# LayerNorm of eight blocks in the convolution's own layout, and raw queries normalised where they are used: a hybrid encoder layer on one core

## The chip, the core and the metric

The kernel runs on one core of a Trainium2 chip. The core's engines run at the same time, each through its own list of instructions in order: PE (TensorE: matrix products and transposes), DVE (VectorE), ACT (ScalarE) and POOL (GpSimd). SP (SyncE) issues all loads and stores of this kernel from one list; 16 DMA engines carry them out. Engines wait for one another by semaphores. SBUF holds tiles of 128 partitions; PE writes its results into PSUM banks of 128 x 512 floats. The metric is the time on the device of one execution, in microseconds (us).

## What is computed

One layer: a first RMSNorm, one projection to seven groups of columns, windowed attention for one half, a convolution with LayerNorm and Silu for the other, gates, and a projection back with a residual. Two sequences of 256 and 2048 rows are 18 blocks of 128 rows.

```python
h = rmsnorm(z, norm_w)
q, k, v, g_att, c_val, c_glu, g_conv = split(h @ w_in)
q = rmsnorm(q by heads, q_norm_w);  k = rmsnorm(k by heads, k_norm_w)
att = windowed_gqa(q, k, v, sink) * silu(g_att)
u = c_val * sigmoid(c_glu)
y = depthwise_conv(u, conv_w, 31 taps) + conv_b
cnv = silu(layernorm(y, ln_w, ln_b)) * silu(g_conv)
out = z + concat(att, cnv) @ w_out
```

## The kernel before

**Stages.** The projection runs over two chunks of the rows, with units of 256 columns that follow one another within a chunk: value and glu of the convolution, the gates, the queries, keys and values. Every product is made in three passes of high and low parts of float32 (`xh`, `xl`), which is why PE is filled. Results that attention needs later go to HBM (`qd` queries, `kd` keys, `vd` values, `gd` gates, `cd` the convolution's output) and are loaded again. In phase 2, which begins within the last queries, the projection's end, the opening of attention and the first products with `w_out` run side by side; after it attention runs alone, in slots: eight slots for each block of 128 rows.

**LayerNorm (`ln_block`).** The convolution leaves `y` with channels on partitions: four tiles of 128 channels. LayerNorm needs sums over channels. So for each block, step `s1` transposes four 128x128 pieces of `y` into a PSUM bank `lnt` (L263), takes mean and variance on DVE (`mv`), and the inverse square root and the shift on POOL (L185, L186, L271). Step `s2` normalises on DVE (`zn`, L281), with rows on partitions. Step `s3` transposes the four pieces of `zn` back (bank `lnu`, L287), and ACT applies weight, bias and Silu (L290); then `zn` is stored to `cd`. `later(n, f)` puts `f` off by n ticks; a tick is a group of matmuls of the main work.

**Queries (`q_group`).** The raw result of a block is copied to a tile `qr` by ACT (L1198), its sum of squares goes to POOL for the inverse root `rqq`, and `fin` multiplies both on DVE (line 490 in the profile, a helper that records the operation) and stores the product to `qd` (L1211). In phase 2 `fin` comes 3 ticks after; for the last four blocks (14 to 17) 10 + 6 x tail ticks more, `put_off`: its products then run at 621 to 676 us, within attention.

**Mixing and output.** Pairs of blocks (p = 0, 1, ...) are taken together, in jobs of sums and differences, each a chain of products into a PSUM bank `yb0` or `yb1` (L755), with tiles `wo0`, `wo1`, ... of the output weights (512 KB a load, L457). A finished bank is added by DVE to the residual in `yo` (`add`, L766) or kept by ACT; the next job that starts the bank waits for it. The tiles `yo0` to `yo3` (256 KB) are loaded by `load_x` (L474) at a slot named in the table `acts`; for the first pair they are at slots 12, 14, 17, 18.

**What sets the order.** Within phase 2 the order on PE and POOL is that of the program. On the other engines, SP's queue among them, a scheduler that simulates the program picks the order, so that a small edit can move a load past others. SP holds its queue while the instruction at the head waits.

## Time and profile before

| | before |
|---|---|
| three runs | 933.9, 935.42, 935.51 us (median 935.42) |
| profiled execution | 935.46 us; span 933.4 |
| bytes moved | 182.79 MB, mean 196 GB/s |
| share of SP's queue in 16 engines' span | 60.0% |

The span is the time from the first to the last recorded instruction; 2.06 us of the execution lie around it. The page cuts the span into 40 slices of 23.3 us; a digit is the busy share in tenths.

```profile
PE   9999999999999999999999999999999999999998
DVE  5799999989988899999996564689788888887884
DMA  8579685488465472223333688998566566576431
GB/s 299 181 226 360 243 287 186 156 272 311 121 211 176 155 290 91 91 99 110 117 116 116 196 268 265 384 361 251 169 171 187 169 200 167 171 187 190 139 96 47
```

Slices 26 and 27 (583 to 630 us) are where DMA moves most: the change of phase. In a row of the timeline stand start, length, engine, line, operation, and in brackets the idle time before it and who ended it.

### The profile page before, as it was taken

The page shows a single profiled execution, that of the slowest core. Times are in us where ns is not written, and L with a number is a line of the kernel's source. Part 1 is how long each engine was busy: PE and PEld are TensorE (multiplying, and loading weights), DVE is VectorE, ACT ScalarE, POOL GpSimd, SP SyncE. Part 2 cuts the span into 40 slices and gives each one's busy share as a digit, 9 for nine tenths or more (in the row PEclk, how much of TensorE's full clock was granted, in tenths as well). Part 3 has the DMA queues.
Part 4 walks back from the last instruction along what each step waited for, and adds up shares of the span by engine and source line. Part 5 has one row for each costly group of instructions (what it writes and reads, how often), then busy time and mean ns, then how long its engine had stood idle before and what let it go on. Part 6 is the DMA issues. An engine that isn't in the chain of part 4 may idle for free.

```text
span 933.4 us, 16976 instructions
## 1 busy us (share of the span) xinstructions
PE 926.0 (99%) x5742; PEld 877.0 (94%) x5742; DVE 786.3 (84%) x1380; ACT 447.6 (48%) x1237; POOL 350.5 (38%) x538
## 2 busy tenths in 40 slices
PE   9999999999999999999999999999999999999998
PEld 8999999999999999999999999988888888888887
DVE  5799999989988899999996564689788888887884
ACT  7441222153447750011111356677667676776772
POOL 3420100075675310000000453676664556455652
PEclk9999999999999999999999999999999999999999
DMA  8579685488465472223333688998566566576431
GB/s 299 181 226 360 243 287 186 156 272 311 121 211 176 155 290 91 91 99 110 117 116 116 196 268 265 384 361 251 169 171 187 169 200 167 171 187 190 139 96 47
DMA packets 154183, 182.79 MB, mean 196 GB/s; under 512 B 48784, under 2 KB 114656, under 8 KB 153968
## 3 DMA queue, kind: packets, MB, share of 16 engines
q1 hardware_dynamic: 154096, 181.71, 60.0%
q8 instruction: 45, 0.74, 0.3%
q14 instruction: 42, 0.34, 0.1%
HBM read 115.81 MB, written 65.85 MB: 195 GB/s over the span
## 4 chain that ended last, share of the span: by engine, by line
PE 97%; DVE 1%; ACT 1%; POOL 1%; issue 0%; DVEq 0%; POOLq 0%
PE pj L1050 43%; PE yb L755 20%; PE pj L1066 16%; PE O L644 5%; PE S L490 4%; PE pT_c L610 2%; PE pT_m L610 2%; PE pT_x L610 1%; PE warmup L1291 1%; PE lnu L287 1%; PE lnt L263 1%; PE qT L490 1%; PE xt L1298 0%; DVE xt L959 0%; DVE y L1131 0%
## 5 line engine op out<-in xcount | busy, mean ns | idle before, releaser
L1050 PE MATMUL pj<-xh,ws 128*128 128x384 f32 (+1 forms) x1536 | 395.4, 338 | 0.1
L1131 DVE SCALAR_TENSOR_TENSOR y<-us,cw,y 128x1167 f32<-128x1167 f32 (+2 forms) x258 | 333.5, 1348 | 0.9
L1050 PEld LDWEIGHTS pj<-xh,ws 128*128 128x128 f32 x1536 | 280.9, 188 | 0.4 <-ACT xh L1306 0.4
L1050 PE MATMUL pj<-xl,ws 128*128 128x384 f32 (+1 forms) x768 | 261.4, 341 | 0.2 <-DVE xl L988 0.2
L1066 PE MATMUL pj<-ws,xh 128*128 128x256 f32 (+1 forms) x880 | 165.4, 284 | 0.7 <-ACT sqq L1179 0.4
L1050 PEld LDWEIGHTS pj<-xl,ws 128*128 128x128 f32 x768 | 144.3, 188 | 0.5 <-DVE xl L988 0.5
L1066 PEld LDWEIGHTS pj<-ws,xh 128*128 128x128 f32 (+1 forms) x880 | 136.5, 187 | 1.4 <-issue 1.0
L755 PE MATMUL yb<-wo,rest 128*128 128x512 f32 (+1 forms) x498 | 132.9, 400 | 0.5 <-DVE rest L490 0.5
L1066 PE MATMUL pj<-ws,xl 128*128 128x256 f32 (+1 forms) x440 | 123.8, 281 | 0.0
L755 PEld LDWEIGHTS yb<-wo,rest 128*128 128x128 f32 x498 | 86.8, 189 | 16.0 <-DVE rest L490 0.9
L580 POOL TENSOR_SCALAR sb<-sb,es 128x304 f32<-128x304 f32 (+4 forms) x144 | 73.0, 525 | 58.4 <-PE pT_x L610 20.6
L1165 ACT ACTIVATE go<-pj 128x384 f32<-128x384 f32 x48 | 23.5, 490 | 147.4 <-PE pj L1050 143.2
L185 POOL TENSOR_SCALAR ssk<-ssk 128x2 f32<-128x2 f32 x18 | 11.8, 657 | 208.2 <-ACT sqk L1179 205.2
L562 ACT ACTIVATE sb<-sb,nm 128x304 f32<-128x304 f32 (+4 forms) x144 | 77.2, 536 | 22.1 <-DVE nm L550 20.2
L550 DVE CUSTOM_DVE_ANT_0 sb<-S,bias,vec 128x304 f32<-128x304 f32 (+4 forms) x144 | 73.3, 510 | 11.4 <-PE S L490 10.4
L1066 PEld LDWEIGHTS pj<-ws,xl 128*128 128x128 f32 (+1 forms) x440 | 82.1, 187 | 0.3
L185 POOL TENSOR_SCALAR ssq<-ssq 128x4 f32<-128x4 f32 (+2 forms) x55 | 27.9, 507 | 99.3 <-ACT xn L913 72.8
L490 PEld LDWEIGHTS S<-kw,q 128*128 128x128 f32 x288 | 52.2, 188 | 11.1 <-ACT rest L490 0.3
L490 PE MATMUL S<-kw,q 128*128 128x304 f32 (+4 forms) x288 | 62.3, 299 | 0.0
L755 PE MATMUL yb<-wo,ptiles 128*128 128x512 f32 x216 | 59.9, 407 | 0.0
L490 POOL TENSOR_TENSOR at<-at,ga 128x256 f32<-128x256 f32 x36 | 27.0, 750 | 79.0 <-DVE at L666 79.0
L766 DVE TENSOR_TENSOR yo<-yb,yo 128x512 f32<-128x512 f32 (+1 forms) x55 | 37.1, 674 | 14.7 <-PE yb L755 14.5
(166 smaller groups left out, 1439.7 us busy)
## 6 DMA issues: line engine op xcount, KB each, us to landing
wd<-ws SPq DMA_DIRECT2D x36, 512.0 KB, 5.8
ws<-wd SPq DMA_DIRECT2D x36, 512.0 KB, 6.1
wraw<-in_w_in SPq DMA_DIRECT2D x52, 256.0 KB, 6.3
xn<-in_z SPq DMA_DIRECT2D x18, 512.0 KB, 5.3
gd<-go SPq DMA_DIRECT2D x48, 192.0 KB, 2.9
yo<-in_z SPq DMA_DIRECT2D x36, 256.0 KB, 3.4
wo<-wod SPq DMA_DIRECT2D x18, 512.0 KB, 7.7
out_y<-yo SPq DMA_DIRECT2D x35, 256.0 KB, 2.3
```

What stands on the lines that cost most here:

```text
L185: nc.gpsimd.tensor_scalar(src, src, scale, eps, op0=ALU.mult, op1=ALU.add)
L490: r = f(*a, **k)
L550: nc.vector.tensor_tensor_reduce(out=sb[:, n, c0:c1], in0=ps[:, 0:w], in1=cst["bias"][:, kv, at + c0 : at + c1], scale=1.0, scalar=nsnk[:, ...
L562: nc.scalar.activation(sb[:, n, c0:c1], sb[:, n, c0:c1], AF.Exp, bias=nm[:, n : n + 1], scale=-1.0, accum_out=rs[:, n : n + 1],)
L580: nc.gpsimd.tensor_scalar(sb[:, k, a0:a1], sb[:, k, a0:a1], es[:, k : k + 1], 1.0, op0=ALU.mult, op1=ALU.mult)
L610: nc.tensor.transpose(pt[: c1 - c0, n, :], sbt[b, kv][:, n, c0:c1], ident)
L644: nc.tensor.matmul(opj[b, kv][:, n0:n1], t, p, start=(k == "c" and i == 0), stop=(k == "x" and i == len(work) - 1),)
L755: nc.tensor.matmul(ps[:, :n], x[mi][:, i, :], w[wi], start=((name, e) in OPENS and k == 0), stop=(done and e == es[-1] and k == 2), skip_g ...
L766: nc.vector.tensor_tensor(y, ps[:, :n], y, op=ALU.add)
L1050: nc.tensor.matmul(ps[:, :n], ws[:, d, wi, P * half_i : P * half_i + P], x[xi][:, d, o : o + n], start=(k == 0), stop=(k == 3 * ND - 1),)
L1066: nc.tensor.matmul(ps[:rows, :UW], x[xi][:, d, o : o + rows], ws[:, d, wi, :], start=(k == 0), stop=(k == 3 * ND - 1),)
L1131: op = nc.vector.scalar_tensor_tensor(y[:, yo + o0 : yo + o1], u[:, o0 + k : o1 + k], cw[:, j, k : k + 1], y[:, yo + o0 : yo + o1], op0=AL ...
```

## The change

For blocks 8 to 15 (`SPREAD`, half-open) LayerNorm is finished in the layout of `y`. `s2` no longer normalises; it transposes two columns of `mv`, each broadcast to 128 columns, so that in a bank every partition holds the 128 rows' factors, and their shifts. `s3` multiplies each of four pieces of `y` by the factors and adds the shifts on DVE; Silu then reads SBUF. For the last four blocks' queries `keep` stores the raw tile one tick after its copy, and `scale_q` multiplies the loaded tile by its `rqq` in slot 3 of the block before.

```diff
+SPREAD = (8, 16)
...
+        spread_b = SPREAD[0] <= b < SPREAD[1]
...
-            later(1, s2)
+            later(2 if spread_b else 1, s2)
 
         def s2():
+            if spread_b:
+                st["rows"] = psum.tile([P, 2, P], F32, tag="d" if phase[0] == 1 else "a", name=f"lnu{b}")
+                for k in range(2):
+                    nc.tensor.transpose(
+                        st["rows"][:, k, :], st["mv"][:, k + 1 : k + 2].to_broadcast([P, P]), ident
+                    )
+                return later(1, s3)
...
         def s3():
-            pt = psum.tile([P, 512], F32, tag="d" if phase[0] == 1 else "a", name=f"lnu{b}")
+            if spread_b:
+                st["zn"] = yp.tile([P, 512], F32, tag="zn", name=f"zn{b}", bufs=4)
+                cn = pt = st["zn"].rearrange("p (j n) -> p j n", n=P)
+                for j in range(NJ):
+                    nc.vector.tensor_tensor(cn[:, j, :], yt[c, j][:, o : o + P], st["rows"][:, 0, :], op=ALU.mult)
+                nc.vector.tensor_tensor(cn, cn, st["rows"][:, 1:2, :].to_broadcast([P, NJ, P]), op=ALU.add)
+            else:
...
+    def scale_q(b):
+        qi, rq = raw_q[b]
+        q = qt[b].rearrange("p a e -> p (a e)")[:, UW * qi : UW * qi + UW].rearrange("p (h e) -> p h e", e=HD)
+        nc.vector.tensor_tensor(q, q, rq.unsqueeze(2).to_broadcast([P, 4, HD]), op=ALU.mult)
...
+        if slot == VSLOT and a + 1 in raw_q:
+            scale_q(a + 1)
...
-                    pin(late and not put_off)(nc.vector.tensor_tensor)(
+                    pin(late)(nc.vector.tensor_tensor)(
...
+                def keep(rq=rq, b=b, raw=raw):
+                    nc.sync.dma_start(qd[b, :, UW * qi : UW * qi + UW], raw.rearrange("p h e -> p (h e)"))
+                    raw_q[b] = (qi, rq)
...
-                later(1 + 2 * late + put_off, fin)
+                if put_off:
+                    later(1, keep)
+                else:
+                    later(1 + 2 * late, fin)
```

The change moves instructions beyond its own lines. A name is a tile with its number, then what is read; lines are those of each kernel's own file (L474 of before is L495 after, L457 is L478, L766 is L787, L755 is L776).

On SP's queue, at the change of phase, before, from the last piece of `wo2` to the load of `yo2`:

```order
L457 DMA wo2_6597<-wod_71 128x1024
L457 DMA wo3_6657<-wod_71 128x1024
L474 DMA yo1_6694<-in_z 128x512
L457 DMA wo3_6657<-wod_71 128x1024 x2
L1211 DMA qd_63<-qr1_13_6456 128x256
L378 DMA q4_7037<-qd_63 128x512
L457 DMA wo5_6881<-wod_71 128x1024
L457 DMA wo4_6780<-wod_71 128x1024
L350 DMA kw1_5913<-kd_65 128x4x32
L457 DMA wo4_6780<-wod_71 128x1024 x2
L474 DMA yo2_6695<-in_z 128x512
```

And after, from the last piece of `wo3` on:

```order
L478 DMA wo3_6676<-wod_71 128x1024
L488 DMA gc3_6963<-gd_64 128x4x128
L488 DMA gc2_7006<-gd_64 128x4x128
L1237 DMA qd_63<-qr1_16_6643 128x256
L392 DMA q4_7055<-qd_63 128x512
L1234 DMA qd_63<-qr1_13_6472 128x256
L478 DMA wo5_6901<-wod_71 128x1024
L478 DMA wo4_6800<-wod_71 128x1024
L364 DMA kw1_5914<-kd_65 128x4x32
L478 DMA wo4_6800<-wod_71 128x1024 x2
L1237 DMA qd_63<-qr1_17_6703 128x256
L495 DMA yo1_6714<-in_z 128x512
```

The load of `yo1` has gone behind everything that stood between it and `yo2`; four raw stores (L1237; those of blocks 14 and 15 stand further up) are newly ahead of it.

On DVE, where the first pair's bank `yb0` is added to `yo1`, before:

```order
L766 TENSOR_TENSOR yo1_6694<-yb0_6725,yo1_6694 128x512 [waits DMAHW3_49,DMAHW1_49,PE_49]
L490 TENSOR_TENSOR rest_6754<-temp1_6768,rest_6754 128x256 [waits Activation_49]
L490 TENSOR_TENSOR rest_6754<-cn0_6262,rest_6754 128x256 [waits DMAHW7_49,Activation_49]
L490 TENSOR_TENSOR ptiles_6207<-cn0_6262,ptiles_6207 128x256 [waits Activation_49]
L666 TENSOR_TENSOR at0_6761<-O0_1_6736,tmp0_1_6858 64x256 [waits Activation_49]
```

and after:

```order
L511 TENSOR_TENSOR rest_6774<-cn1_6274,rest_6774 128x256 [waits Activation_49]
L640 SCALAR_TENSOR_TENSOR ptiles_6223<-pT1_x_0_6890,vec_77,ptiles_6223 128x128 [waits Activation_49]
L640 SCALAR_TENSOR_TENSOR ptiles_6223<-pT1_x_0_6890,vec_77,ptiles_6223 128x128
L511 TENSOR_TENSOR rest_6774<-at0_6781,rest_6774 128x256 [waits Activation_49]
L787 TENSOR_TENSOR yo1_6714<-yb0_6745,yo1_6714 128x512 [waits DMAHW0_49]
L571 ISA sb1_5926,nm2_0_6818<-S2_0_2_6898,bias_5910,vec_77 128x240 [waits PE_49]
```

The addition has moved down past the whole block of `cn0`, `at0` and `cn1`, behind the product with `at0`, and directly waits for a load (DMAHW).

On PE, the job that starts `yb0` anew with `wo1`, before and after:

```order
L606 MATMUL pT1_x_0_6870<-ident_72,pm1_0_6715 128x128 [waits PE_49,Pool_49]
L755 MATMUL yb0_6725<-wo1_6429,ptiles_6207 128x512 [waits Activation_49]
L755 MATMUL yb0_6725<-wo1_6429,ptiles_6207 128x512
L755 MATMUL yb0_6725<-wo1_6429,ptiles_6207 128x512 [waits DVE_49]
L755 MATMUL yb0_6725<-wo2_6597,ptiles_6207 128x512 [waits DMAHW6_49]
```

```order
L627 MATMUL pT1_x_0_6890<-ident_72,pm1_0_6735 128x128 [waits PE_49,Pool_49]
L776 MATMUL yb0_6745<-wo1_6445,ptiles_6223 128x512 [waits DVE_49,Activation_49]
L776 MATMUL yb0_6745<-wo1_6445,ptiles_6223 128x512 x2
L776 MATMUL yb0_6745<-wo2_6615,ptiles_6223 128x512 [waits DMAHW4_49]
L776 MATMUL yb0_6745<-wo2_6615,ptiles_6223 128x512 [waits DMAHW5_49]
```

The job stands at the same place; its first matmul now waits for DVE too, for the count at which the addition above is done.

Also on PE, where block 8's rows are transposed, after:

```order
L265 MATMUL lnt9_5479<-ident_72,y1_3_4745 128x128
L1089 MATMUL pj132_5503<-ws1_8_4971,xh5_3593 128x256 [waits PE_49,Activation_49]
L1089 MATMUL pj132_5503<-ws1_8_4971,xl5_3594 128x256
L1089 MATMUL pj132_5503<-ws1_8_4971,xh5_3593 128x256 x2
L1089 MATMUL pj132_5503<-ws1_8_4971,xl5_3594 128x256
L1089 MATMUL pj132_5503<-ws1_8_4971,xh5_3593 128x256 x2
L1089 MATMUL pj132_5503<-ws1_8_4971,xl5_3594 128x256
L284 MATMUL lnu8_5494<-ident_72,mv8_5428 128x128 [waits DVE_49,Pool_49]
```

Before, `lnu8` waited for DVE (its `zn8`) some eight projection matmuls further down; now it waits for POOL as well.

## The prediction

> **What bounds the kernel now.** First the page: the busy line, then the chain that ended last.

> ```profile
> PE 926.0 (99%) x5742; PEld 877.0 (94%) x5742; DVE 786.3 (84%) x1380; ACT 447.6 (48%) x1237; POOL 350.5 (38%) x538
> PE 97%; DVE 1%; ACT 1%; POOL 1%; issue 0%; DVEq 0%; POOLq 0%
> ```

> TensorE is the bound: 97% of the last chain is PE, and it idles 7 us in the whole span. So anything can only gain by taking PE time away, and anything that makes PE wait costs its full length. Next I cut the span at the stages that the change touches: the rest of the projection with the LayerNorm of chunk 1 (520 to 583 us), the change of phase (581 to 621), and attention up to where the last raw queries will be used. Columns: stretch, length, busy time of PE, PEld, DVE, ACT, POOL, granted clock, DMA share, GB/s.

> ```profile
> 520.00:583.00 63.00, 63.00 (x541) 63.00 (x541) 34.51 (x96) 33.25 (x112) 30.25 (x71) 1.00 0.78 236
> 575.00:578.00 3.00, 3.00 (x28) 3.00 (x27) 1.78 (x5) 0.58 (x3) 1.59 (x5) 1.00 0.41 100
> 581.00:621.00 40.00, 39.38 (x289) 36.46 (x288) 30.32 (x89) 27.61 (x85) 26.90 (x54) 1.00 1.05 386
> 615.30:700.00 84.70, 84.34 (x467) 71.81 (x466) 72.80 (x194) 59.50 (x161) 56.38 (x90) 1.00 0.74 221
> 700.00:840.00 140.00, 140.00 (x792) 120.92 (x791) 118.16 (x308) 100.65 (x263) 75.26 (x107) 1.00 0.64 180
> ```

> PE is full in all of them at a granted clock of 1.00. In the first one DVE and ACT are only a bit over half busy. The third row matters most: for 40 us the DMA engines are full (share 1.05 at 386 GB/s), so there a transfer lands by the bytes ahead of it. Three microseconds before that stretch fills, the share was 0.41.

> **Term 1: PE's transposes.** For blocks 8 to 15 four transposes of zn back become two of the broadcast columns of mv. How much a transpose costs PE is not its duration but the distance to the next start.

> ```profile
> L287 PE MATMUL lnu<-ident,zn x72: 270/272/273, 289.1 to 570.6; 128*128 128x128 f32 x72
> ...
> 540.27 0.28 PE L1066 MATMUL pj<-ws,xl 128*128 128x256 f32 x1
> 540.38 0.60 PE L287 MATMUL lnu<-ident,zn 128*128 128x128 f32 x4
> 540.74 0.36 PE L1066 MATMUL pj<-ws,xh 128*128 128x256 f32 x1
> 540.94 0.60 PE L263 MATMUL lnt<-ident,y 128*128 128x128 f32 x4
> 541.29 0.36 PE L1066 MATMUL pj<-ws,xh 128*128 128x256 f32 x1
> 541.50 0.28 PE L1066 MATMUL pj<-ws,xl 128*128 128x256 f32 x1
> ```

> One lasts 272 ns, but four overlap to 0.60 us. From the start of the group to the next matmul is 0.36 us, and that one then takes 0.20 us to the next start where 0.12 is its own pitch (540.27 to 540.38 reads 0.11): 0.36 + 0.20 - 0.12 = 0.44 us for four, 0.11 us each. Eight blocks x 2 fewer x 0.11 = **1.76 us saved**. By durations it would be 16 x 0.272 = 4.35 us. [...]

> **Term 2: the normalising on DVE and ACT.** A zn of 0.81 us goes; four 128x128 multiplications and one 128x512 addition come.

> ```profile
> L281 DVE TENSOR_SCALAR zn<-lnt,mv 128x512 f32<-128x512 f32 x18 | 14.5, 808 | 8.8 <-POOL mv L271 6.7 <-POOL rqq L186 1.8
> L766 DVE TENSOR_TENSOR yo<-yb,yo 128x512 f32<-128x512 f32 (+1 forms) x55 | 37.1, 674 | 14.7 <-PE yb L755 14.5
> 538.96 0.29 DVE L1224 TENSOR_TENSOR vs<-pj,vs 128x128 fp32r<-128x128 f32 x1
> ```

> 4 x 0.29 + 0.67 = 1.83 us, so 1.0 us more per block, 8 us in all, beside a DVE that idles 63 - 34.5 = 28 us in that stretch. Nothing on PE waits for it: Silu and a store follow. Cost 0; without the cover, at most those 8 us. Silu reading SBUF in place of PSUM is ACT's, which has 30 us free: 0.

> **Term 3: PE now waits for POOL's mv.** Before, PE's transposes waited for DVE's zn; now they wait for the last POOL step of mv itself, one tick later in PE's order (`later 2`).

> ```profile
> 529.87 0.60 PE L263 MATMUL lnt<-ident,y 128*128 128x128 f32 x4
> ...
> 532.96 0.27 POOL L271 TENSOR_SCALAR mv<-mv 128x1 f32<-128x1 f32 x1
> ```

> mv8 is ready 533.23 - 529.87 = 3.4 us after lnt8 begins. In the new order lnu8 stands behind lnt9 and about nine more projection matmuls, by PE's rows of before some 4.4 us after lnt8. Queued behind a late one would be projection matmuls, and everything after them. Bounds: 0, and 0.5 us for the tightest block (14, whose mv stands on POOL behind other work). I take 0.

> **Term 4: the raw queries' multiplication moves.** Four DVE operations (qr<-qr,rqq) go from 621 to 676 us to slots at some 822, 841, 860 and 878 us; they are the same size.

> ```profile
> 621.00 0.43 DVE L490 TENSOR_TENSOR qr<-qr,rqq 128x256 f32<-128x256 f32 x1
> ...
> 801.95 1.29 SPq L378 DMA_DIRECT2D q<-qd  x1
> ...
> 829.27 0.60 PE L490 MATMUL qT<-ident,q 128*128 128x128 f32 x4
> ```

> The load of such a q is issued 27 us ahead of the transposes that use it, so the product finds its data. Each adds 0.42 us to a DVE that is busy 118 of 140 us: no PE wait follows, cost 0; bound 4 x 0.42 = 1.7 us with no cover. The four stores of 128 KB move from after 621 us into the full stretch: that is term 5.

> **Term 5, the decisive one: a load on SP's queue.** SP issues in the order that the scheduler sets, and this moved. The load of yo1 (256 KB, the residual that DVE adds at L766) stood ahead of q4, kw1, the rest of wo3 and the first of wo4 and wo5. Now it stands exactly where yo2 stood: what is set ahead of the new yo1, counted from the first gate load of this stage, is what was set ahead of the old yo2, plus four raw stores.

> ```profile
> 604.18 0.91 SPq L474 DMA_DIRECT2D yo<-in_z  x1
> ...
> 614.29 0.33 SPq L474 DMA_DIRECT2D yo<-in_z  x1
> ...
> DMA to landing us min/median/max: 7.1/7.3/7.5
> ...
> 621.45 1.29 POOL L784 TENSOR_TENSOR yo<-yo,keptFalse 128x512 f32<-128x512 f32 x1 [0.35 <-DMA yo<-in_z]
> ```

> The old yo1 lands at 604.18 + 7.5 = 611.7, the old yo2 at 614.29 + 7.1 = 621.4, which the POOL row confirms (it had waited for it). New yo1: 621.4 + 4 x 131 KB / 386 GB/s (4 x 0.34 = 1.36) - yo2's own 0.68 = 622.1. The other way round: six pieces of 524 KB, q4, kw1, the store of block 13 and the four raw stores, 4.13 MB, are newly ahead of it; 4.13 MB / 386 GB/s = 10.7, and 611.7 + 10.7 = 622.4. I take 622.2 by before's clock.

> Who waits: the addition of yo1 on DVE, and behind it on PE the job that starts bank yb0 anew and needs that very addition done.

> ```profile
> 612.41 0.68 DVE L766 TENSOR_TENSOR yo<-yb,yo 128x512 f32<-128x512 f32 x1
> ...
> 613.01 0.46 DVE L490 TENSOR_TENSOR rest<-temp,rest 128x256 fp32r<-128x256 f32 x1
> ...
> 613.53 1.21 PE L755 MATMUL yb<-wo,rest 128*128 128x512 f32 x4 [0.48 <-DVE rest L490]
> 615.29 0.94 PE L755 MATMUL yb<-wo,ptiles 128*128 128x512 f32 x3
> ```

> Before, the addition was done at 613.09 and PE began the job at 615.29 without a wait. The waking of PE by DVE takes 613.53 - 613.47 = 0.06 us. After: landing + 0.68 + 0.06.

> Does term 1 shift the landing? The stream fills at 578 us, from a share of 0.41 just before, and what lets it start are buffers that the projection frees. PE gets there 1.76 us sooner by then (the last LayerNorm is over at 572), so I take the whole stream as that much sooner: landing 620.44, PE goes on at 621.2 rather than 615.29, **+5.9 us**. If the stream doesn't shift, the landing is 622.2 and it is +7.65. If all of it flows at 409 GB/s, as its best five microseconds do, its 44 us are 2.4 shorter, +3.5.

> ```profile
> 605.00:610.00 5.00, 4.86 (x32) 4.08 (x32) 4.20 (x15) 4.12 (x12) 2.98 (x8) 1.00 1.04 409
> ```

> What of it comes back: PE idles 84.70 - 84.34 = 0.36 us from 615.3 to 700 and nothing up to 840, so at most **-0.3**. Term 1 is already inside the landing: whatever PE saves before 615 is waited away at that place.

> **The sum.** The profiled execution took 935.46 us (span 933.4 and 2.06 around it), within 0.04 of the median of 935.42. 935.46 + 5.9 - 0.3 = **941.1 us**. Own range of this case: 938.7 (fast stream) to 942.8 (no shift).

> **Rivals.** *A: the load is hidden, PE never waits.* Then only term 1 is left: 935.46 - 1.76 = 933.7. It decides if yo1 lands by 612.8 us (PE due at 615.29 - 1.76 = 613.53, less 0.74) and DVE comes to the addition by then. Against it: 7.1 us from issue to landing for both yo loads, and DVE's order (next rival). 4%.

> *B: yo1 overtakes the large transfers and lands on time; then DVE's own order decides.* [...] The landings of before, 7.1 to 7.5 us for yo amid loads of 524 KB, show no overtaking. But even so the addition now stands behind a product with at0 which before ran here:

> ```profile
> 617.83 0.61 DVE L490 TENSOR_TENSOR rest<-at,rest 128x256 fp32r<-128x256 f32 x1
> ```

> It ends at 618.4, or from 616.1 with the shift and the rows between gone; plus 0.74, PE starts at 616.8 to 619.2: 935.46 + 1.5 - 0.3 = 936.7 up to 939.0. 11%.

> *C: longer.* The wait leaves DVE, ACT and SP with late work behind it (DVE's next softmax operations stand behind the addition), or a raw store holds SP's queue because ACT's copy is late. For the second speaks

> ```profile
>   DMA qd<-qr: 3.9, 2
> ```

> (copies into qr waited twice for a store); against it, a hold shorter than the 7 us of transfers in flight lets no DMA engine run dry. One piece of 524 KB more ahead is 1.36 us, so one to three of them: 942.5 to 945.2. 11%.

> *That the transposes don't get cheaper* (broadcast columns costing PE more than plain ones) changes nothing here, as term 1 is waited away, except through the shift: 942.8, inside the main range.

> **How the numbers follow.** Main case 74%, A 4%, B 11%, C 11%. To leave out no more than two in ten I reach from the low end of B to nearly the far end of C: 936.7 to 945.0. A measurement of this kernel can tell about 0.2% (1.9 us) from no change. Faster than that: A, 4%. Within (933.6 to 937.3): the low end of B, 5%. Slower: 91%.

> **What would show it.** A PE wait of 5 to 8 us near 614 us, put down to the addition of yo<-yb on DVE, and on DVE a wait of some 3 us for DMA yo<-in_z: right. PE's rows at 575 us sooner by 1.8 us: term 1; by more than 3: the durations counted after all. A wait of lnu on POOL's mv: term 3. If PE runs through at 614 us, terms 1 to 4 alone decide and I am wrong by 7 us; if the idle time stands at another line, the order of SP was misread.

## The result, and the profile after

| | before | after |
|---|---|---|
| median | 934.82 us (6 runs, 933.9 to 935.55) | 944.38 us (6 runs, 940.71 to 944.72) |
| profiled execution | 935.46 us, span 933.4 | 944.58 us, span 942.8 |
| ratio after / before | | 1.0094, 95% interval 1.0077 to 1.0111 |

The change costs 0.94% by the means of the runs (8.8 us) and 9.6 us by their medians; predicted were 941.1 us, with a range of 936.7 to 945.0. The page's busy line and chain, after:

```profile
PE 926.2 (98%) x5726; PEld 875.5 (93%) x5726; DVE 789.6 (84%) x1412; ACT 447.6 (47%) x1237; POOL 352.8 (37%) x538
PE 91%; DMA 4%; DVE 2%; ACT 1%; issue 1%; POOL 1%; SPq 0%; DVEq 0%; POOLq 0%; ACTq 0%
```

PE issues 16 matmuls fewer, yet is as long busy as before: something made others slower. And 4% of the chain that ended last is now DMA, where it had none worth a percent. PE's waits, from the view of who waited for whom (total, times, longest, in us):

```profile
PE yb L776 <- DVE yo L787: 6.6, 1, 6.6
...
PE pj L1089 <- ACT sqq L1197: 1.7, 1, 1.7
PE O L665 <- DVE ptiles L646: 1.0, 3, 0.6
PE lnu L304 <- DVE zn L290: 0.7, 1, 0.7
```

The first is the predicted one. The waits on `sqq` (ACT's squares of a raw query, which stand behind its copy) and on `zn` come before it, at 595 and 571 us. The place of the first in the timeline, on SP, DVE and PE:

```profile
614.68 0.81 SPq L495 DMA_DIRECT2D yo<-in_z  x2
...
617.56 1.12 DVE L511 TENSOR_TENSOR rest<-at,rest 128x256 fp32r<-128x256 f32 x1 [0.62 <-ACT rest L511]
621.43 0.69 DVE L787 TENSOR_TENSOR yo<-yb,yo 128x512 f32<-128x512 f32 x1 [2.75 <-DMA yo<-in_z]
...
615.36 0.27 PE L627 MATMUL pT_x<-ident,pm 128*128 128x128 f32 x1
622.27 2.90 PE L776 MATMUL yb<-wo,ptiles 128*128 128x512 f32 x6 [6.64 <-DVE yo L787]
624.97 0.61 PE L511 MATMUL S<-kw,q 128*128 128x240 f32 x2
...
628.34 0.41 PE L511 MATMUL S<-kw,q 128*128 128x272 f32 x2
```

SP issues the load of yo1 (the first of the two) at 614.68, where before it stood at 604.18. DVE came to the addition at 618.7 and waited for the landing until 621.43; PE had stood since 615.63 and goes on at 622.27. So the late place of the addition in DVE's own order accounts for some 3.9 us of PE's wait, and the landing for the last 2.75.

PE's row at 622.27 shows what the prediction lacked. The six matmuls of that job take 2.90 us; before, they took 1.63:

```profile
615.29 1.63 PE L755 MATMUL yb<-wo,ptiles 128*128 128x512 f32 x6
```

Next the stretches from the stop on. Their columns are start and end, length, busy times of PE, PEld, DVE, ACT, POOL, then granted clock, DMA share, GB/s:

```profile
615.63:619.00 3.37, 0.00 (x1) 0.00 (x0) 2.25 (x6) 1.47 (x5) 3.28 (x6) 1.00 1.04 393
619.00:620.50 1.50, 0.00 (x0) 0.00 (x0) 0.00 (x0) 0.00 (x0) 1.33 (x3) 1.00 1.06 383
620.50:621.00 0.50, 0.00 (x0) 0.00 (x0) 0.00 (x0) 0.00 (x0) 0.50 (x1) 0.93 1.19 317
621.00:622.00 1.00, 0.00 (x0) 0.00 (x0) 0.56 (x1) 0.00 (x0) 0.33 (x2) 0.50 1.21 314
622.00:627.50 5.50, 5.23 (x13) 4.23 (x14) 0.60 (x3) 0.59 (x2) 1.27 (x1) 0.50 1.01 363
627.50:628.50 1.00, 1.00 (x6) 0.83 (x5) 0.00 (x0) 0.00 (x0) 0.00 (x0) 0.87 1.03 387
```

The granted clock falls to 0.50 some 5 us after PE stopped, and PE then works at 0.50 for over 5 us before it is 1.00 again. In "busy" this looks like work.

To see where the rest went, one can follow the same instruction through both traces: the transposes qT, once for each block. Before, then after:

```profile
601.55 0.60 PE L490 MATMUL qT<-ident,q 128*128 128x128 f32 x4
625.62 0.60 PE L490 MATMUL qT<-ident,q 128*128 128x128 f32 x4
811.41 0.60 PE L490 MATMUL qT<-ident,q 128*128 128x128 f32 x4
885.75 0.60 PE L490 MATMUL qT<-ident,q 128*128 128x128 f32 x4
```

```profile
601.88 0.60 PE L511 MATMUL qT<-ident,q 128*128 128x128 f32 x4
635.13 0.60 PE L511 MATMUL qT<-ident,q 128*128 128x128 f32 x4
819.93 0.60 PE L511 MATMUL qT<-ident,q 128*128 128x128 f32 x4
895.57 0.60 PE L511 MATMUL qT<-ident,q 128*128 128x128 f32 x4
```

Later by 0.33, 9.51, 8.52 and 9.82 us: nothing is gained by 601, 9.2 us are lost at the yo1 wait and in the slow stretch behind it, 1.0 comes back, and 1.3 are lost again between 811 and 886 (by the clock of before), where the raw queries are multiplied.

### The profile page after: what moved, and what is told of

It is laid out like the page before. It is cut to its first block, busy times and chain, and to the rows that moved or that the text cites. A ratio compares the mean times of both kernels' runs of the same rounds, so it can differ in the third digit from the quotient of the medians.

```text
span 942.8 us, 16977 instructions
## 1 busy us (share of the span) xinstructions
PE 926.2 (98%) x5726; PEld 875.5 (93%) x5726; DVE 789.6 (84%) x1412; ACT 447.6 (47%) x1237; POOL 352.8 (37%) x538
## 4 chain that ended last, share of the span: by engine, by line
PE 91%; DMA 4%; DVE 2%; ACT 1%; issue 1%; POOL 1%; SPq 0%; DVEq 0%; POOLq 0%; ACTq 0%
PE pj L1073 43%; PE yb L776 19%; PE pj L1089 13%; PE O L665 5%; PE S L511 4%; PE pT_c L631 2%; PE pT_m L631 2%; DMA q<-qd 1%; PE pT_x L631 1%; DMA bias<-in_bias_c 1%; PE qT L511 1%; DMA yo<-in_z 1%; PE lnt L265 1%; DMA xn<-in_z 1%; DMA cd<-zn 0%
## 5 line engine op out<-in xcount | busy, mean ns | idle before, releaser
L776 PE MATMUL yb<-wo,rest 128*128 128x512 f32 (+1 forms) x498 | 133.3, 402 | 0.0
L776 PEld LDWEIGHTS yb<-wo,rest 128*128 128x128 f32 x498 | 87.6, 190 | 15.4
L186 POOL TENSOR_SCALAR ssk<-ssk 128x2 f32<-128x2 f32 x18 | 12.0, 668 | 207.1 <-ACT sqk L1202 203.0
L776 PE MATMUL yb<-wo,ptiles 128*128 128x512 f32 x216 | 61.2, 413 | 6.6 <-DVE yo L787 6.6
L186 POOL TENSOR_SCALAR ssq<-ssq 128x4 f32<-128x4 f32 (+2 forms) x55 | 27.8, 506 | 101.6 <-ACT xn L936 69.6
L776 PEld LDWEIGHTS yb<-wo,ptiles 128*128 128x128 f32 x216 | 38.7, 192 | 14.4 <-issue 7.0
```

Source lines behind the costliest of these rows:

```text
L186: nc.gpsimd.tensor_scalar(src, src, scale, eps, op0=ALU.mult, op1=ALU.add)
L776: nc.tensor.matmul(ps[:, :n], x[mi][:, i, :], w[wi], start=((name, e) in OPENS and k == 0), stop=(done and e == es[-1] and k == 2), skip_g ...
```

## The experiments

The theory after this: four losses. The load of yo1 (6.6 us of waiting); the half clock that follows a long wait (2.5); the waits at 571 and 595 us, which eat term 1; and DVE's standing still for the raw q (1.3). The rivals: the LayerNorm's operations themselves, or the change of phase being late as a whole.

### e1 and e2: each part alone

e1 (first) keeps the LayerNorm part and takes the queries back; e2 (second) the other way round:

```diff
-                    pin(late)(nc.vector.tensor_tensor)(
+                    pin(late and not put_off)(nc.vector.tensor_tensor)(
-                if put_off:
-                    later(1, keep)
-                else:
-                    later(1 + 2 * late, fin)
+                later(1 + 2 * late + put_off, fin)
```

```diff
-SPREAD = (8, 16)
+SPREAD = (18, 18)
```

> Only the LayerNorm part; the last queries are put off and stored as before the change. The load of yo1 has 9.3 MB ahead of it in this stage (14.0 MB with the whole change). If the place of that load decides (theory): it lands near 609 us, no wait of PE on the addition to yo1, granted clock 1.00 at 622 to 628, time near that of before: 1.8 us of transposes saved, against the waits at 571 us (0.7, block 16's transposes) and 595 us (1.7, the late store of a query tile), which stay because wo0 and wo1 are still ahead of that store: 934 to 936. If the LayerNorm's operations on DVE themselves cost the time (rival): 940 or more, with PE waits at DVE's line in 520 to 583.

> Only the raw queries; LayerNorm as before. The load of yo1 has 12.9 MB ahead of it: 1.1 MB less than with the whole change. Theory: landing near 619, PE waits some 4 us at the job that starts yb0 anew; if the clock falls only after some 5 us of idle time (it fell about that long after PE stopped), it stays at 1.00 or falls for less; 0.25 us more for the DVE waits of scale_q up to 1.3: 938 to 942. Rival (both parts needed, or the waits at 571 and 595 are the start of it): near 935.

Measured: e1 934.64 us beside 934.79 before (ratio 0.9998, 0.9988 to 1.0008). yo1 is issued at 599.37 and nobody waits for it. Of PE's waits between 560 and 640 us two are left:

```profile
PE pj L1089 <- ACT sqq L1197: 1.8, 1, 1.8
PE O L665 <- DVE ptiles L646: 0.8, 1, 0.8
```

e2 942.27 us (ratio 1.0080, 1.0065 to 1.0095), a little above the range I had given. The load of yo1 is issued at 612.03, later than before without the LayerNorm part too, and

```profile
617.39 0.69 DVE L787 TENSOR_TENSOR yo<-yb,yo 128x512 f32<-128x512 f32 x1 [0.55 <-DMA yo<-in_z]
...
613.72 0.27 PE L627 MATMUL pT_x<-ident,pm 128*128 128x128 f32 x1
618.23 2.90 PE L776 MATMUL yb<-wo,ptiles 128*128 128x512 f32 x6 [4.24 <-DVE yo L787]
```

PE waits 4.24 us and again needs 2.90 us for the six matmuls: the half clock comes after a shorter wait than I thought. Of that wait the landing is only 0.55 us; the rest is DVE coming late to the addition, which here too stands behind a product with `at`. So the raw queries' part alone moves the load and the addition behind; the LayerNorm part alone doesn't. The rival that LayerNorm's work on DVE costs time falls.

### e3: only the load of yo1 earlier

```diff
-            (9 + 3 * (p == 0), lambda p=p: load_x(p, (0, 1))),
+            (9 + 1 * (p == 0), lambda p=p: load_x(p, (0, 1))),
```

> The whole change, and the load of yo1 two slots earlier in the table: on SP's queue it then stands behind the raw store of block 15, 3.8 MB further up, and nothing else moves there. Theory: it lands near 611.5, the wait of 6.6 us goes and with it the half clock after it (2.5 us): 944.4 - 9.1 = 935.3. Rival (the 40 us of full DMA engines are late as a whole, and the wait moves to the next load): the wait appears at another line, 940 or more.

Measured: 937.38 us (1.0023, 1.0012 to 1.0035): 7 us of the change's 9.6 gone, 2 us less than expected. The job starts without a wait, and its six matmuls take 1.64 us:

```profile
605.10 0.33 SPq L495 DMA_DIRECT2D yo<-in_z  x1
...
617.40 1.64 PE L776 MATMUL yb<-wo,ptiles 128*128 128x512 f32 x6
...
620.95 0.41 PE L511 MATMUL S<-kw,q 128*128 128x272 f32 x2
```

From the job's start to the scores S of 128x272 it takes 3.55 us here; with the whole change it took 6.07 (622.27 to 628.34): the half clock cost 2.5 us. What was missed shows earlier. The wait on sqq was longer in this execution (2.77 us; 1.71 with the whole change), and the clock fell there:

```profile
595.74 0.58 PE L1089 MATMUL pj<-ws,xh 128*128 128x256 f32 x1 [2.77 <-ACT sqq L1197]
...
592.75:595.74 2.99, 0.22 (x3) 0.01 (x1) 0.64 (x5) 0.72 (x3) 2.74 (x6) 0.99 1.05 394
595.74:599.20 3.46, 3.46 (x16) 3.46 (x17) 2.79 (x9) 2.77 (x10) 3.38 (x7) 0.52 1.09 395
```

The edit moves the load's row up on SP; the scheduler then also moves the addition up on DVE (it runs at 615.53, without a wait). The two aren't told apart.

### e4: the raw queries multiplied later and held in order

On top of e3:

```diff
-        if slot == VSLOT and a + 1 in raw_q:
+        if slot == 5 and a + 1 in raw_q:
...
-        nc.vector.tensor_tensor(q, q, rq.unsqueeze(2).to_broadcast([P, 4, HD]), op=ALU.mult)
+        pin(True)(nc.vector.tensor_tensor)(q, q, rq.unsqueeze(2).to_broadcast([P, 4, HD]), op=ALU.mult)
```

> As the last, and scale_q two slots later, held in program order on DVE, so that DVE doesn't stand still for the landing of q (8.6 us in four waits with the whole change). Theory: PE's pitch between 800 and 900 us, 1.3 us worse than before with the whole change, comes back: 1 to 1.3 us less than e3, near 934. Rival (those waits are covered by DVE's idle time and the 1.3 us come from the products' place): the same as e3.

Measured: 934.19 us (0.9993, 0.9983 to 1.0003), no different from before; its ten runs lie far apart, from 931.98 to 936.39. DVE no longer waits for q, which with the whole change it did for 8.6 us in four waits:

```profile
  DMA q<-qd: 8.6, 4
```

The difference to e3 is 3.2 us, more than expected. In the profiled execution the wait at 595 was 2.39 us and left the clock alone: the matmuls `pj<-ws,xl` behind it took 0.28 us each, where in e3 they took 0.41 to 0.42. By my estimate that accounts for some 2 us of the difference (0.4 of the wait, and about 1.7 for e3's 3.3 us of PE's work at a clock of 0.50). e5 and e7 compare without this wait.

### e5 to e8: the wait at 595

ACT's copy of a raw query, ahead of `sqq`, waits there (3.31 us with the whole change, 3.40 in e1, put down to DMA qd<-qr) for the store of the tile whose buffer it takes, that of block 17's first half, which stood behind three loads of wo. The edit, on e4 (e5), e1 (e6), e3 (e7) and the kernel before (e8), makes that product and its store come sooner (in e6 and e8 the last line keeps its `+ put_off`):

```diff
-                rq = head_norm(ps, P, 4, f"q{qi}_{b}", 2 * late + put_off)
+                rq = head_norm(ps, P, 4, f"q{qi}_{b}", 2 * late + put_off - ((qi, b) == (0, 17)))
...
-                    later(2 - late, lambda: nc.sync.dma_start(to, qs.rearrange("p h e -> p (h e)")))
+                    st = lambda: nc.sync.dma_start(to, qs.rearrange("p h e -> p (h e)"))
+                    st() if (qi, b) == (0, 17) else later(2 - late, st)
...
-                    later(1 + 2 * late, fin)
+                    later(1 + 2 * late - ((qi, b) == (0, 17)), fin)
```

> As e4, and the query of block 17's first half is multiplied and stored one or two ticks sooner: on SP's queue its store stands 2.3 MB further up, ahead of four loads of wo. Theory: the buffer that ACT's copy waits for at 592 to 595 us is free some 5 us sooner, and PE's wait on sqq there (1.7 to 3.0 us in the kernels with the LayerNorm part) goes: e4's 934.2 less 2.4 is near 931.8. Rival (the wait moves on to the next copy, or to the load of yo1, which stands 0.5 MB later than in e4): 933.5 or more with a PE wait at another line.

> As e1 (the LayerNorm part alone), with the same earlier store. Theory: PE's wait of 1.8 us near 594 goes, and the 1.76 us of the transposes are left: 934.6 - 1.9 = 932.7. If the transposes save nothing: 934.6 or, with the wait gone, no lower than 934.0.

> As e3 with the same earlier store; scale_q is not held in order. Against e5 it tells what DVE's waits for q cost apart from the wait at 595: theory 1.0 to 1.5 us more than e5, near 933. Rival (covered): equal to e5.

> The kernel before with the same earlier store alone. There ACT's copy waited 1.5 us near 592, and PE didn't wait for it. Theory: no change, 934.5 to 935.1. Rival (the earlier store is a gain by itself): 933 or less.

| | median | ratio to before | 95% interval |
|---|---|---|---|
| e5 | 934.85 us | 1.0001 | 0.9992 to 1.0010 |
| e6 | 933.37 us | 0.9985 | 0.9976 to 0.9994 |
| e7 | 936.02 us | 1.0017 | 1.0008 to 1.0026 |
| e8 | 934.15 us | 1.0001 | 0.9992 to 1.0010 |

The wait on sqq is gone in all. e6 is as expected within 0.7 us: the LayerNorm part alone, with its store in time, is the only version whose interval lies below 1, by 0.15%. Term 1 can be read off here: its qT against that of e8, the same kernel but for LayerNorm.

```profile
598.78 0.60 PE L511 MATMUL qT<-ident,q 128*128 128x128 f32 x4
```

```profile
600.52 0.60 PE L490 MATMUL qT<-ident,q 128*128 128x128 f32 x4
```

600.52 - 598.78 = 1.74 us, and both begin chunk 0's transposes at the same 288.1 us. In the medians of the two (933.37 and 934.15) 0.8 us of it is left. e8 shows that the earlier store is no gain by itself.

e5 went the rival's way: the time did not fall below e4's. In place of the wait stand others behind it, most of them for ACT's work on `ptiles`:

```profile
PE O L665 <- ACT ptiles L645: 0.8, 1, 0.8
PE yb L776 <- ACT ptiles L638: 0.6, 1, 0.6
PE O L665 <- DVE ptiles L646: 0.4, 2, 0.2
```

e7 is 1.2 us slower than e5, the difference that was expected (the time itself is 3 us above the 933 that was): that is what DVE's waits for q cost. In e7 DVE stood 12.3 us for q, and from its qT at 811.33 to the one four blocks later, at 888.38, are 77.05 us; in e5 from 809.76 to 884.58 it is 74.82.

### e9: two blocks more

```diff
-SPREAD = (8, 16)
+SPREAD = (8, 18)
```

> As e6, with blocks 16 and 17 too (SPREAD to 18): four transposes fewer, 0.44 us by the pitch of 0.11. Theory: 933.4 - 0.4 = 933.0, unless the waits on POOL's mv show now: POOL has the queries' sums at that place; each would be up to 1 us. On SP's queue the load of yo1 has 9.7 MB ahead of it, as early as in the kernel before, so no wait there. Rival (the place of the loads in the change of phase decides more than the transposes): 933.8 or more.

Measured: 935.14 us (1.0007, 0.9998 to 1.0016), so slower than e6, the rival's way; runs lay between 933.29 and 937.0. No wait on POOL's mv shows. In the profiled execution, the fastest of the eleven, the wait at the change of phase was

```profile
PE yb L776 <- DVE rest L511: 0.9, 1, 0.9
```

against 0.2 in e6. Why most runs were slower than that execution stays open.

## Why the prediction was right, step by step

**Term 5, the decisive step, was right in mechanism and close in size.** Predicted: the load lands at 620.44, PE goes on at 621.2. Measured: 621.4 and 622.27. The miss of 1 us lies within the assumed shift: I let the whole stream start 1.76 us sooner because PE would; but PE's lead was eaten by waits at 571 and 595 before, as its qT at 601.88 shows. Without shift I had 622.2, and the landing lies between. How much of the stream did shift isn't shown.

**Term 1 was right**: 1.76 us predicted, 1.74 measured between e6 and e8. The pitch of 0.11 us was the right price and not the duration of 0.27, by which it would have been 4.35.

**Term 2 was right**: the additions took 0.68 and the multiplications 0.28 us each on DVE, and no wait of PE in that stretch is put down to them (e1).

**Term 3 was right for mv**: no transposition of mv waits for POOL in PE's list. But DVE now waits for buffers of zn whose stores are late: 4.8 us at block 15's and 0.6 at block 17's, the last of the list (the expectation of e1 calls it block 16's), and PE 0.7 us for the latter. The prediction had no such step.

**Term 4 was wrong in one reading.** "The load of such a q is issued 27 us ahead of the transposes that use it" joined the load at 801.95 to the wrong qT: those that use it are at 811.41, 9.5 us behind. And DVE came to the first product at 811.28, 0.85 us after its load was issued (810.43), and stood 2.76 us. So DVE waited for the landings, 8.6 us in all, and PE lost 1.3 us. That lies within the 1.7 I had named as the bound without cover, but by chance: that bound was four products at 0.42 us, not a wait for a load.

**Missing from the sum: the clock.** Costing a wait of PE at its own length left out 2.5 us. In three traces the granted clock fell from 1.00 to 0.50 during a wait of PE and came back during the work behind it. The half clock lasted 6.8 us with the whole change and in e2, and 3.4 in e3:

```profile
620.93:627.75 6.82, 5.48 (x14) 4.44 (x15) 1.17 (x3) 0.59 (x2) 1.67 (x3) 0.50 1.04 356
617.14:623.96 6.82, 5.73 (x15) 4.61 (x16) 1.17 (x3) 0.59 (x2) 3.46 (x5) 0.50 1.07 372
595.65:599.07 3.42, 3.33 (x15) 3.34 (x16) 2.69 (x9) 2.86 (x11) 3.34 (x7) 0.50 1.10 393
```

PE had stopped 5.3, 3.2 and 2.7 us before. So here a gap of 2.77 us (e3) was enough, while 2.39 in e4 and 1.80 in e1 left the clock alone (`pj<-ws,xl` behind them: 0.28 us in e4, 0.28 to 0.29 in e1).

**The sum, with what was measured.** In the profiled executions PE goes on 7.0 us later than before (622.27 against 615.29), loses 2.5 at the half clock, gets 1.0 back by 820 us, loses 1.3 for the raw queries and gets 0.4 back behind them; 0.3 less lies around the span. 935.46 + 7.0 + 2.5 - 1.0 + 1.3 - 0.4 - 0.3 = 944.6, beside 944.58. What PE won or lost ahead of 615 us isn't in this sum, since the landing swallows it.

**What came back was 1.0 us, not 0.3.** Most of it lies between the qT at 640.05 and at 699.82 (by the clock of before): 59.77 us before, 58.90 with the change and 58.97 in e2, but 60.09 in e1, where the put-off products still run on DVE in that stretch. So it goes with the raw queries' part. The prediction took PE's idle time as the bound; but PE's busy time shrank too, from 59.41 to 58.86 us for the same 329 matmuls.

**The rivals, and luck.** A did not happen. B's reading of DVE's order was more than half of the truth: DVE came to the addition at 618.7, 0.3 us behind the 616.1 to 618.4 given there, and only then waited for the load. That the load would overtake what was ahead of it doesn't show: it took 6.7 us from issue to landing, as did the last piece of wo and the last raw store ahead of it. With the load in time PE would, by my estimate, have gone on near 619.5, 3.9 us behind its stop. C's reasons (late work after the wait, a held queue) show in no long wait of PE. The measured 944.4 lies outside the main case's own range (938.7 to 942.8). It is within 936.7 to 945.0 only because the range was stretched for C, and what filled that place was the clock, which the prediction did not have. So the mechanism was right, and that the time fell within the range was in part luck.

## What to carry to other kernels

Where a scheduler sets a queue's order, read what an edit moves past what: here a change that saves 1.7 us of matmuls cost 9.6, since a 256 KB load had gone behind 4.1 MB in a stretch where the DMA engines were full (share 1.05 at 386 GB/s), and the addition that uses it behind other work of DVE. A wait of PE can cost more than its length: in this case the clock fell to 0.50 at waits of 2.77, 4.24 and 6.64 us, and not at 2.39, and behind the longest that was 2.5 us more. And an operation that uses a loaded tile needs its place held well behind the load, or the engine's whole list stands for it: here DVE stood 8.6 us in four waits for q.
